# Ordered recurrence: the first chunk's preparation goes inside the hand-ordered part, its inverse and its operand from DRAM are emitted later, and the planner's delays get longer

## The chip, the cores and the metric

The kernel runs on one core of one Trainium2 chip. The metric is the device time of one execution in microseconds (us), smaller is better. In the profile the engines are PE (TensorE matmuls) and PEld (its weight loads), DVE (VectorE), ACT (ScalarE), POOL (GpSimd) and SP (SyncE, which here issues most DMAs).

## The reference: two layers of a hybrid trunk

512 latent tokens and 256 context tokens of width 1024 pass two layers. Layer 0 mixes tokens with four mLSTM heads and eight RWKV-7 heads, layer 1 with RG-LRU and neighbourhood attention; a squared-ReLU MLP follows each mixer. The change touches only RWKV-7 of layer 0, which the reference writes as a scan over single tokens, in both directions z:

```
S = S * w_t + (S a_t) b_t + v_t k_t      # 64 x 64 state of one head
y_t = S r_t
```

w, k, b come from the input projection through low-rank maps; context runs first and its last state starts the latent scan.

## The kernel before: how the work is tiled and ordered

Channels lie on the 128 partitions, tokens along the free dimension. A product with a weight matrix (`gemm`, L290) takes weight tiles of 128x1024, split in a high part `wh` (ACT, L283) and a low part `wl` (POOL or DVE, L287) of the fast matmul type; each output block `psg` is 24 matmuls (xh.wh, xl.wh, xh.wl). `psg` has two PSUM banks in this stage.

**The scan in chunks.** RWKV-7 is computed in 12 chunks of 64 tokens (4 of context, 8 of latent), all 8 heads and both directions at once. A chunk s is prepared, without the state, by two generators:

- `front(s)` (L934) loads `bk`, `ar`, `AS`, `X` from DRAM and forms the chunk's 64x64 products in `psA`, from which ACT and DVE write `AB`, `AS`, `Q`.
- `back(s)` (L968) inverts the unit triangular matrix of each head and direction. Its 16x16 diagonal blocks go through DRAM (`AB` to `dA`, L975; `dA` to `M`, L981), 15 elimination steps of two operations each run on them (L995, L997; on POOL for s up to 4, on DVE for the later ones), and the blocks go out and back in another layout (`Xi` to `invD`, L1000; `invD` to `Xr`, L1002). DVE transposes `Xr` to `Xt` (L1005). Four groups of small matmuls `psI` then merge the 16x16 inverses to 64x64 (`dd`, `t2`, `t3`, `d1`, `T`).

`step(s)` (L1076) carries the state over one chunk with four groups of matmuls `psC`, and `chain` (L1068) calls it for s = 0 to 11.

**The order of the work.** Up to L1276 a scheduler with a modelled clock orders every engine. In this first part the last action before the ordered part is letter "R" of a string (L1224), after which mLSTM head 3 still has two pieces to run. Under "R" the kernel before calls `front(0)` and `back(0)` to the end, so that chunk 0 is prepared among the instructions of head 3, with one PSUM bank for `psA`.

The ordered part (from `ordered[0] = True`, L1276) fixes the order of PE by hand. The main generator `fillers` issues large products: `rwkv_in(1)`, the 15 input projections of the latent tokens, with the four `operands` generators that turn them into the scan's operands; then half of the latent output projection, the context's gate and output projection, and the context MLP. After each matmul a planner's clock `now` is advanced by the matmul's planned time (`mm`, L170), and `poll` (L139) lets any generator whose due time has come emit its next piece: `chain` in queue "step", `prepare(1)` and `prepare(0)` in queues "odd" and "even", `operands` in "in", the context gate in "gate". A generator's `yield 3.0` means: due again 3.0 us of `now` later; a `yield lambda` means: due when the condition holds. A pair of conditions orders the chunks: `front(s)` starts when `keys[0] == s - 1` and enough steps are done (`free`, L1058), and chunks 4 and later wait for `"in"`, the end of `rwkv_in(1)`. The ordered part ends when step 11 has been emitted; what is left of the context MLP then runs beside the last gate.

Only PE follows this order. ACT, DVE, POOL and the DMA queues are ordered by the scheduler's modelled clock, each runs strictly in that order, and an instruction whose operand is late holds all behind it.

Of the kernel before, what the change touches and what calls it, by code (L numbers as in the profile page):

```python
# [14 lines left out]
ALU = mybir.AluOpType  # L15
# [3 lines left out]
P = 128  # L19
# [11 lines left out]
NCR = T // CR  # L31
# [86 lines left out]
def hybrid_kernel(ctx: ExitStack, tc: tile.TileContext, A, out):  # L118
# [623 lines left out]
    def rwkv_in(si, psp, psh, tag, last=None, tail=None):  # L742
# [5 lines left out]
        with tc.tile_pool(name=nm("pha"), bufs=1) as pha, tc.tile_pool(name=nm("ph"), bufs=1) as ph, \  # L748
# [34 lines left out]
            def operands(p, T):  # L783
# [12 lines left out]
                    ups.append((uh, ul))  # L796
                sq = pha.tile([P, n], F32, tag="sq", name=nm("sq"))
                nc.scalar.activation(c64(sq), k, AF.Square, scale=V["k_k"][:, p:p + 1])
                yield 4.2
                pst = psh.tile([P, nb, 2], F32, tag=tag, name=nm("pst"))  # L800
                for c in range(nb):
                    mm(pst[:, c, :], sq[:, P * c:P * c + P], C["hsel"])
# [4 lines left out]
                rx = ph.tile([P, nb, P], F32, tag="sh", name=nm("rx"))  # L807
                nc.scalar.copy(rx.rearrange("p c (h i) -> p (c h) i", h=2),
                               rk.rearrange("p c h -> p (c h)")[:, :, None].to_broadcast([P, 2 * nb, 64]))
                yield 2.6  # L810
                bc = psh.tile([P, nch, 64], F32, tag=tag, name=nm("psbc"))
                for c in range(nb):
                    mm(bc[:, 2 * c:2 * c + 2, :], rx[:, c, :], ident)
# [2 lines left out]
                for z in range(2):  # L816
                    uh, ul = ups[z]
                    for kind in range(2):
                        yield 1.2
                        pw = psh.tile([P, nch, 64], F32, tag=tag, name=nm("psw"))  # L820
                        mm(fl(pw), uh[:, kind, :], low[kind][z], True, False)
                        mm(fl(pw), ul[:, kind, :], low[kind][z], False, True)
                        t_ = ph2.tile([P, nch, 64], F32, tag=f"th{kind}", name=nm("th"))
                        o = 8 * z + 4 * kind + p
                        nc.scalar.activation(t_, pw, AF.Tanh, scale=0.5, bias=DV["upb"][:, o:o + 1])
                        th.append(t_)
# [107 lines left out]
    def front(s):  # L934

        ch = chunk_of(s)
        si, s0 = (0, 0) if s < 4 else (1, 4)
        pr2, X = set_of(s), new_x(s)
        ar = pr2.tile([P, 2, 4, P], F32, tag="ar", name=nm("ar"))
        bk = pr.tile([P, 2, 4, P], F32, tag="bk", name=nm("bk"))  # L940
        Q = pr2.tile([P, 2, 4, 2, 64], F32, tag="Q", name=nm("Q"))
        AS = pr2.tile([P, 2, 4, 2, 64], F32, tag="AS", name=nm("AS"))
        AB = pr.tile([P, 2, 4, 64], F32, tag="AB", bufs=2, name=nm("AB"))
        nc.sync.dma_start(bk, bkD[si][:, s - s0])
        nc.sync.dma_start(ar, arD[si][:, s - s0])
        for q in range(2):
            nc.sync.dma_start(AS[0:64, :, :, q, :], arD[si][hs_[q], s - s0, :, :, 0:64])
        for z in range(2):
            c = 64 * (ch[z] - s0)
            nc.sync.dma_start(X[64:P, z].rearrange("t p q i -> t (p q i)"), vD[si][c:c + 64].rearrange("t p i -> t (p i)"))  # L950
        yield 13.0 if s == CT // CR else 9.0
        for z in range(2):

            pa_ = [None, None]
            for heads in (((0, 1),) if banks["A"][2] > 1 else ((0,), (1,))):
                for q in heads:
                    pa_[q] = bank("A", [P, 4, P])
                for p in range(4):
                    for q in heads:
                        mm(pa_[q][:, p, :], bk[hs_[q], z, p, :], ar[hs_[q], z, p, :])  # L960
                for q in heads:
                    nc.scalar.copy(AB[hs_[q], z], pa_[q][0:64, :, 0:64])
                    nc.vector.tensor_tensor(AS[64:P, z, :, q, :], pa_[q][64:P, :, 0:64], amask(z, 0, HI), op=ALU.mult)
                    nc.vector.tensor_tensor(Q[:, z, :, q, :], pa_[q][:, :, 64:P], amask(z, 1, FULL), op=ALU.mult)
            yield 3.0
        FRONT[s] = (ar, bk, Q, AS, AB, pr2)

    def back(s):  # L968
# [17 lines left out]
        for z in range(2):  # L986
            pt = bank("A", [P, 4, P])
            for p in range(4):
                transpose(pt[:, p, :], bk[:, z, p, :])
            nc.scalar.copy(BK[:, z], pt)  # L990
        eng = nc.gpsimd if s <= CT // CR else nc.vector
        for j in range(15):
            n, m = 15 - j, j + 1
            t_ = tm[:, 0:n, 0:m]
            eng.tensor_tensor(t_, M[:, m:16, j:j + 1].to_broadcast([64, n, m]),  # L995
                              Xi[:, j:j + 1, 0:m].to_broadcast([64, n, m]), op=ALU.mult)
            eng.tensor_tensor(Xi[:, m:16, 0:m], Xi[:, m:16, 0:m], t_, op=ALU.add)  # L997
        for k in range(4):
            dst = bass.AP(tensor=dX.tensor, offset=dX.offset + 512 * k + 16 * (k % 2), ap=[[2048, 16], [32, 16], [1, 16]])
            nc.sync.dma_start(dst, Xi[16 * k:16 * k + 16])  # L1000
        Xr = pr.tile([P, 8, 32], F32, tag="Xr", bufs=2, name=nm("Xr"))
        nc.sync.dma_start(Xr, dX.rearrange("u p t -> p u t"))  # L1002
        Xt = pr.tile([P, 8, 32], F32, tag="Xt", bufs=2, name=nm("Xt"))
        fl8 = lambda a: a.rearrange("p a b -> p (a b)")
        nc.vector.transpose(fl8(Xt), fl8(Xr))  # L1005
        keys[0] = s
        yield 33.0
        yield lambda: merged[0] == s - 1

        tt = (Xt[:, 0:4], Xr[:, 4:8])  # L1010
# [5 lines left out]
                    mm(pi[b32[g], z, p, :], AB[b32[g], z, p, b32[g % 2]], ti[z][b32[g], p, :], tile=(g, g))  # L1016
        dd = pr.tile([P, 2, 4, 32], F32, tag="dd", name=nm("dd"))
        nc.vector.tensor_tensor(dd, pi, lmask, op=ALU.mult)
        yield 1.4
        pj = bank("I", [P, 2, 4, 32])  # L1020
        for z in range(2):
            for p in range(4):
# [8 lines left out]
        T = pr2.tile([P, 2, 4, 64], F32, tag="T", name=nm("T"))  # L1031
        for b in range(2):
            nc.scalar.activation(T[:, :, :, b32[b]], t2, AF.Copy, scale=C["bsel"][:, b:b + 1])
        yield 2.4
        pi = bank("I", [P, 4, 32])
        for p in range(4):
            for z, q in ((0, 0), (1, 0), (0, 1), (1, 1)):
# [1 line left out]
                mm(pi[b32[o], p, :], AB[b32[g], z, p, b32[1 - z]], t3[b32[g], z, p, :], tile=(g, o))  # L1039
        d1 = pr.tile([P, 4, 32], F32, tag="d1", name=nm("d1"))  # L1040
        nc.scalar.copy(d1, pi)
        yield 1.2
        pj = bank("I", [P, 4, 32])
        for p in range(4):
            for z, q in ((0, 0), (1, 0), (0, 1), (1, 1)):
# [4 lines left out]
            nc.vector.scalar_tensor_tensor(t_, pj, C["bsel"][:, z:z + 1], t_, op0=ALU.mult, op1=ALU.add)  # L1050
        tt = (T[:, 0], T[:, 1])
        merged[0] = s
        yield 2.0
        PRE[s] = (ar, GE[:, s], Q, AS, BK, tt)

    seen = set()
# [3 lines left out]
        return steps[0] >= s - (1 if s <= CT // CR else 2) and (s < CT // CR or "in" in done)  # L1060

    def prepare(parity):
        for s in range(2 - parity, NCR, 2):
            yield lambda: free(s) and keys[0] == s - 1
            yield from front(s)
            yield from back(s)

    def chain(S):  # L1068
        for s in range(NCR):
            yield lambda: s in PRE and (s < CT // CR or "lat" in done)  # L1070
            S = yield from step(s, new_x(s), S, new_x(s + 1) if s + 1 < NCR else None)
            rwkv_norms(s)
            steps[0] = s + 1
            yield 3.6

    def step(s, X, S0, Xn):  # L1076
        ar, ge, Q, AS, BK, tt = PRE.pop(s)
        chunk = chunk_of(s)
        pR = bank("C", [P, 2, 4, 64])
        for z, p, q in UNITS:  # L1080
            mm(pR[hs_[q], z, p, :], AS[:, z, p, q, :], X[:, z, p, q, :])
        r_ = pr.tile([P, 2, 4, 64], F32, tag="r", name=nm("r"))
        nc.scalar.copy(r_, pR)
        yield 1.5
        pU = bank("C", [P, 2, 4, 64])
        for z, p, q in UNITS:
            mm(pU[hs_[q], z, p, :], tt[z][hs_[q], p, :], r_[hs_[q], z, p, :])
        nc.scalar.copy(X[0:64, :, :, 0, :], pU[0:64])
        nc.vector.tensor_copy(X[0:64, :, :, 1, :], pU[64:P])
        yield 2.0  # L1090
        S1 = None
        if s < NCR - 1:
            pS = bank("C", [P, 2, 4, 64])
            for z, p, q in UNITS:
                mm(pS[hs_[q], z, p, :], BK[:, z, p, hs_[q]], X[:, z, p, q, :])
            S1 = set_of(s + 1).tile([P, 2, 4, 64], F32, tag="S", name=nm("S"))
            nc.vector.tensor_tensor(S1, pS, S0, op=ALU.add)
            nc.vector.tensor_tensor(S1, S1, ge[:, :, :, None].to_broadcast([P, 2, 4, 64]), op=ALU.mult)
            nc.scalar.copy(Xn[0:64, :, :, 0, :], S1[0:64])
            nc.vector.tensor_copy(Xn[0:64, :, :, 1, :], S1[64:P])  # L1100
        pY = bank("C", [P, 2, 4, 64])
        first = [None, None]
        for z, p, q in UNITS:
            i1 = mm(pY[hs_[q], z, p, :], Q[:, z, p, q, :], X[:, z, p, q, :], first[q] is None, False, shared=True)
            if first[q] is None:
                first[q] = i1
            else:
                after(i1, first[q])
        for z, p, q in UNITS:
            mm(pY[hs_[q], z, p, :], ar[hs_[q], z, p, 64:P], S0[hs_[q], z, p, :], False, False, shared=True)  # L1110
        for z in range(2):
            d = ya_of(chunk[z])
            if chunk[z] in seen:
                nc.vector.tensor_tensor(d, pY[:, z], d, op=ALU.add)
            else:
                seen.add(chunk[z])
                nc.scalar.copy(d, pY[:, z])
        return S1
# [105 lines left out]
    for o in "0000a0c1ccc1cc11c1c22cc2c23c12ccc33cR33":  # L1224
# [3 lines left out]
        elif o == "R":  # L1228
# [5 lines left out]
            pr = st_r.enter_context(tc.tile_pool(name="pr", bufs=1))  # L1234
            add_set()
            inv += [pr.tile([P, 16, 16], F32, name=a) for a in ("M", "Xi", "tm")]
            banks.update(A=(psh2, "h", 1), I=(psa1, "ada", 1))
            S = sets[0].tile([P, 2, 4, 64], F32, tag="S", name="S0")
            nc.vector.memset(S, 0.0)
            nc.vector.memset(new_x(0)[0:64], 0.0)  # L1240
            for _ in front(0):
                pass
            for _ in back(0):
                pass
        else:
            next(work[o], None)
    assert all(next(w, 0) == 0 for w in work.values())
# [373 lines left out]
```

## Time and profile before

| | us |
|---|---|
| median of 3 runs (2118.84 to 2122.49) | 2121.51 |
| the profiled execution's own time | 2113.17 |
| its span, first to last instruction | 2111.3 |
| PE busy (share of the span) | 1932.4 (92%) |
| PEld busy | 1591.6 (75%) |
| DVE busy | 1079.3 (51%) |
| ACT busy | 874.6 (41%) |
| POOL busy | 869.4 (41%) |

Busy time is the union of an engine's instructions. The mean granted clock of PE over the span was 0.956 of full speed. In the list of stretches the ordered part lies from about 406 to 996 us. A number in square brackets at the end of a row is the engine's idle time just before that instruction, and what ended it.

### The profile page before, as it was taken

How to read it: one execution, taken by the hardware profiler on the slowest of the kernel's cores; microseconds unless marked ns; L12 is line 12 of the kernel's file. 1: busy time of each engine (PE TensorE's matmuls, PEld its weight loads, DVE VectorE, ACT ScalarE, POOL GpSimd, SP SyncE). 2: the span in 40 equal slices, each digit the busy share in tenths (PEclk: the TensorE clock that was granted, in tenths of full speed). 3: DMA queues.
4: the chain of work that ended last, by engine and by line, in shares of the span. 5: the costliest groups of instructions: out<-in, count | busy, mean ns of one | idle time of the engine just before them, and what ended most of it. 6: DMA issues, size and time to landing. Idle time of an engine off the chain costs nothing. (4 is left out here: it accounts for less than half of the span.)

```text
span 2111.3 us, 36782 instructions
## 1 busy us (share of the span) xinstructions
PE 1932.4 (92%) x14924; PEld 1591.6 (75%) x14924; DVE 1079.3 (51%) x1947; ACT 874.6 (41%) x1444; POOL 869.4 (41%) x706
## 2 busy tenths in 40 slices
PE   6899997587877889889999999999999999999998
PEld 5788875465656878878877888888666678888887
DVE  6764545268765676676652212234567655122222
ACT  4444544254544434434442323334555655233232
POOL 1456545254435221222434444434454363444444
PEclk9999998698988898999999999999999999999999
DMA  8355657345376454543453233334211032333322
GB/s 307 101 203 201 213 189 238 79 112 152 106 237 187 125 154 134 154 125 111 133 191 124 86 105 95 100 100 152 68 60 41 28 103 70 93 97 100 97 94 80
DMA packets 171929, 271.62 MB, mean 129 GB/s; under 512 B 75056, under 2 KB 113584, under 8 KB 166640
## 3 DMA queue, kind: packets, MB, share of 16 engines
q1 hardware_dynamic: 166704, 263.76, 39.9%
q10 hardware_dynamic: 5056, 5.51, 0.8%
q8 instruction: 118, 1.93, 0.4%
q14 instruction: 51, 0.42, 0.1%
HBM read 244.06 MB, written 25.17 MB: 128 GB/s over the span
## 5 line engine op out<-in xcount | busy, mean ns | idle before, releaser
L287 POOL TENSOR_TENSOR wl<-w,wh 128x1024 fp32r<-128x1024 f32 (+3 forms) x245 | 555.3, 2269 | 816.1 <-PE psg L172 477.5
L283 ACT CAST wh<-w 128x1024 fp32r<-128x1024 f32 (+3 forms) x319 | 313.8, 986 | 527.9 <-PE psg L172 421.0
L172 PE MATMUL psg<-xh,wh 128*128 128x512 f32 (+1 forms) x1440 | 504.3, 364 | 18.6 <-DVE y L385 6.5
L172 PE MATMUL psg<-xl,wh 128*128 128x512 f32 (+1 forms) x1440 | 506.1, 363 | 0.8 <-DVE xl L388 0.7
L172 PEld LDWEIGHTS psg<-xh,wh 128*128 128x128 f32 x1440 | 277.4, 194 | 73.4 <-issue 19.9
L172 PE MATMUL psg<-xh,wl 128*128 128x512 f32 (+1 forms) x1440 | 331.8, 358 | 0.0
L172 PEld LDWEIGHTS psg<-xl,wh 128*128 128x128 f32 x1440 | 279.5, 194 | 46.5 <-issue 7.3
L172 PEld LDWEIGHTS psg<-xh,wl 128*128 128x128 f32 x1440 | 244.4, 192 | 41.4 <-issue 6.8
L172 PE MATMUL psg<-hh,wh 128*128 128x512 f32 (+1 forms) x800 | 267.6, 352 | 6.0 <-DVE res_c L391 3.3
L172 PE MATMUL psg<-hl,wh 128*128 128x512 f32 (+1 forms) x800 | 268.7, 352 | 0.6 <-DVE hl L334 0.6
L391 DVE SCALAR_TENSOR_TENSOR res_l<-psg,mod,res_l 128x512 f32<-128x512 f32 (+1 forms) x108 | 74.2, 689 | 276.6 <-PE psg L172 276.6
L172 PEld LDWEIGHTS psg<-hh,wh 128*128 128x128 f32 x800 | 153.1, 193 | 26.9 <-issue 3.0
L172 PEld LDWEIGHTS psg<-hl,wh 128*128 128x128 f32 x800 | 152.8, 193 | 20.4 <-DVE hl L334 0.8
L172 PE MATMUL psg<-hh,wl 128*128 128x512 f32 (+1 forms) x800 | 166.7, 349 | 0.0
L436 DVE TENSOR_SCALAR r<-psg 128x512 f32<-128x512 f32 (+1 forms) x96 | 57.3, 600 | 179.2 <-PE psg L172 178.8
L172 PEld LDWEIGHTS psg<-hh,wl 128*128 128x128 f32 x800 | 132.9, 191 | 19.1
L334 DVE TENSOR_TENSOR hl<-r,hh 128x512 fp32r<-128x512 f32 (+1 forms) x96 | 93.1, 974 | 86.2 <-ACT hh L333 86.0
L437 ACT ACTIVATE r<-r 128x512 f32<-128x512 f32 (+1 forms) x96 | 53.4, 559 | 133.1 <-DVE r L436 133.1
L287 DVE TENSOR_TENSOR wl<-w,wh 128x1024 fp32r<-128x1024 f32 (+1 forms) x74 | 93.4, 1262 | 29.5 <-ACT wh L283 23.4
L172 PE MATMUL psada<-adaw,sc 128*32 128x256 f32 (+1 forms) x896 | 62.2, 382 | 10.9 <-DMA adaw<-in_ada_w_dram 6.9
L333 ACT CAST hh<-r 128x512 fp32r<-128x512 f32 (+1 forms) x96 | 52.6, 550 | 2.7
L995 POOL TENSOR_TENSOR tm<-M,Xi 64x15 f32<-64x15 f32 (+7 forms) x75 | 26.9, 358 | 62.4 <-DMA M<-dA 57.5
(421 smaller groups left out, 2871.7 us busy)
## 6 DMA issues: line engine op xcount, KB each, us to landing
w<-in_w_dram SPq DMA_DIRECT2D x192, 512.0 KB, 3.6
adaw<-in_ada_w_dram SPq DMA_DIRECT2D x40, 1024.0 KB, 6.9
w<-in_ev_in_dram SPq DMA_DIRECT2D x47, 512.0 KB, 3.7
w<-in_od_in_dram SPq DMA_DIRECT2D x32, 512.0 KB, 3.6
adaw<-in_ada_dram SPq DMA_DIRECT2D x16, 512.0 KB, 11.2
w<-in_out_w_dram SPq DMA_DIRECT2D x32, 256.0 KB, 3.5
ar<-arD SPq DMA_DIRECT2D x12, 512.0 KB, 4.4
bk<-bkD SPq DMA_DIRECT2D x12, 512.0 KB, 5.0
```

The costliest lines, as they stand in the source:

```text
L172: ins = nc.tensor.matmul(o, l, r, start=start, stop=stop, skip_group_check=shared, **kw)
L283: nc.scalar.copy(wh, w)
L287: eng.tensor_tensor(wl, w, wh.bitcast(F32), op=ALU.subtract)
L333: nc.scalar.copy(h, x)
L334: nc.vector.tensor_tensor(l, x, h.bitcast(F32), op=ALU.subtract)
L391: nc.vector.scalar_tensor_tensor(r_, ps, modcol(layer, idx, m, cnd), r_, op0=ALU.mult, op1=ALU.add)
L436: nc.vector.tensor_scalar(r_, ps, 0.0, None, op0=ALU.max)
L437: nc.scalar.activation(r_, r_, AF.Square)
L995: eng.tensor_tensor(t_, M[:, m:16, j:j + 1].to_broadcast([64, n, m]), Xi[:, j:j + 1, 0:m].to_broadcast([64, n, m]), op=ALU.mult)
```

## The change

Eleven delays of the planner get longer, in `operands`, in the merge of `back`, in `front` and in `step`. `front(0)` and `back(0)` are no longer called under "R"; instead queue "even" starts at chunk 0, so that chunk 0 is prepared inside the ordered part like the others, with two banks for `psA` (the branch for one bank goes). In `back`, the single delay of 33 is divided: 8 after the block-transposes of `bk`, then the elimination in three groups of five steps with 3 between them, then 14 before the transpose of `Xr`, and 1 after it. `tc.keep_in_program_order` pins the first operation of each group, and the transpose, behind everything emitted before on the same engine.

```diff
@@ operands @@
-                yield 4.2
+                yield 4.6
...
-                yield 2.6
+                yield 3.6
...
-                        yield 1.2
+                        yield 1.8
@@ front @@
-            yield 3.0
+            yield 3.4
@@ back @@
+        keys[0] = s
+        yield 8.0
         eng = nc.gpsimd if s <= CT // CR else nc.vector
         for j in range(15):
+            if j in (5, 10):
+                yield 3.0
...
-            eng.tensor_tensor(t_, M[:, m:16, j:j + 1]...
+            ins = eng.tensor_tensor(t_, M[:, m:16, j:j + 1]...
+            if j in (0, 5, 10):
+                tc.keep_in_program_order(ins)
...
+        yield 14.0
         Xt = pr.tile([P, 8, 32], F32, tag="Xt", bufs=2, name=nm("Xt"))
-        nc.vector.transpose(fl8(Xt), fl8(Xr))
-        keys[0] = s
-        yield 33.0
+        tc.keep_in_program_order(nc.vector.transpose(fl8(Xt), fl8(Xr)))
+        yield 1.0
         yield lambda: merged[0] == s - 1
...
-        yield 1.4 / 2.4 / 1.2 / 2.0      # the merge's four
+        yield 2.4 / 4.0 / 1.8 / 2.6
@@ prepare @@
-        for s in range(2 - parity, NCR, 2):
+        for s in range(parity, NCR, 2):
@@ chain and step @@
-            yield 1.5 / 2.0 / 3.6
+            yield 2.2 / 3.0 / 4.2
@@ under "R" @@
-            banks.update(A=(psh2, "h", 1), I=(psa1, "ada", 1))
-            for _ in front(0):
-                pass
-            for _ in back(0):
-                pass
```

(The lines with several numbers stand for one line each.)

## Rows read from the trace of the kernel before

**Rows 1.** Stretches: length, busy us (instructions) PE PEld DVE ACT POOL, PEclk, DMA, GB/s.
```profile
340.00:1060.00 720.00, 592.76 (x7485) 514.25 (x7485) 470.03 (x928) 297.67 (x533) 244.86 (x313) 0.89 0.49 143
...
410.00:620.00 210.00, 174.44 (x1831) 134.01 (x1830) 146.67 (x222) 100.26 (x175) 90.22 (x148) 0.90 0.48 141
...
380.00:390.00 10.00, 1.54 (x6) 1.14 (x6) 1.18 (x3) 1.04 (x3) 7.74 (x25) 0.50 0.42 128
390.00:400.00 10.00, 0.29 (x20) 0.29 (x24) 0.31 (x1) 0.00 (x0) 3.89 (x14) 0.50 0.24 46
400.00:410.00 10.00, 7.05 (x225) 6.07 (x217) 2.10 (x7) 1.76 (x4) 0.00 (x0) 0.50 0.04 9
...
450.00:460.00 10.00, 4.94 (x16) 4.27 (x17) 3.25 (x6) 3.56 (x5) 1.33 (x6) 0.67 0.55 126
...
550.00:560.00 10.00, 2.80 (x12) 2.03 (x11) 4.76 (x7) 2.31 (x4) 3.25 (x5) 0.79 0.24 46
```

**Rows 2.** Timeline of PE around chunk 0: start, length, engine, line, operation [idle before].
```profile
327.04 0.58 PE L172 MATMUL psg<-xh,wh 128*128 128x512 f32 x1
...
363.88 1.40 PE L172 MATMUL psA<-ar,bk 64*128 64x128 f32 x8 [2.24 <-issue]
...
381.66 1.54 PE L736 MATMUL pst<-cst,hall 128*128 128x128 f32 x6 [2.27 <-POOL hall L731]
...
399.71 0.65 PE L172 MATMUL psI<-Xr,AB 32*32 32x32 f32 x32 [16.51 <-DMA Xr<-invD]
...
408.08 0.80 PE L172 MATMUL psg<-xl,wh 128*128 128x512 f32 x1
```

**Rows 3.** Timeline of POOL: first and last elimination operation of chunks 0 and 1.
```profile
382.09 0.22 POOL L995 TENSOR_TENSOR tm<-M,Xi 64x15 f32<-64x15 f32 x1 [0.48 <-DMA M<-dA]
...
393.88 0.21 POOL L997 TENSOR_TENSOR Xi<-Xi,tm 64x15 f32<-64x15 f32 x1
...
433.15 0.73 POOL L995 TENSOR_TENSOR tm<-M,Xi 64x15 f32<-64x15 f32 x1 [35.23 <-DMA M<-dA]
...
446.49 0.22 POOL L997 TENSOR_TENSOR Xi<-Xi,tm 64x15 f32<-64x15 f32 x1
```

**Rows 4.** Waits of DVE, 405 to 1060 us: total, times, longest.
```profile
DVE Xt L1005 <- DMA Xr<-invD: 36.6, 10, 8.0
DVE tm L995 <- DMA M<-dA: 18.5, 6, 6.8
```

**Rows 5.** Timeline of DVE: the three longest of these waits.
```profile
453.62 0.45 DVE L1005 STREAM_TRANSPOSE Xt<-Xr 128x256 f32<-128x256 f32 x1 [7.59 <-DMA Xr<-invD]
...
555.10 0.45 DVE L1005 STREAM_TRANSPOSE Xt<-Xr 128x256 f32<-128x256 f32 x1 [7.97 <-DMA Xr<-invD]
...
908.55 0.18 DVE L995 TENSOR_TENSOR tm<-M,Xi 64x15 f32<-64x15 f32 x1 [6.84 <-DMA M<-dA]
```

**Rows 6.** Timeline of PE: the three longest stalls between 420 and 1050 us.
```profile
455.06 2.08 PE L172 MATMUL psbc<-cst,rx 128*128 128x128 f32 x8 [5.24 <-ACT rx L808]
...
559.55 0.79 PE L172 MATMUL psw<-low,uh 128*128 128x512 f32 x1 [7.20 <-ACT th L825]
...
911.89 1.97 PE L172 MATMUL psC<-r,T 64*64 64x64 f32 x32 [5.77 <-ACT r L1083]
```

**Rows 7.** Waits of PE, 420 to 1050 us: total, times, longest.
```profile
PE psI L172 <- DVE dd L1018: 10.5, 4, 3.8
PE psC L172 <- DVE X L1089: 8.2, 4, 3.7
```

**Rows 8.** Timelines of ACT and PE: steps 4 and 6, the last step, the fill's end.
```profile
723.78 0.58 ACT L1083 COPY r<-psC 128x512 f32<-128x512 f32 x1
...
804.16 0.59 ACT L1083 COPY r<-psC 128x512 f32<-128x512 f32 x1
...
995.97 1.15 PE L172 MATMUL psC<-S,ar 64*64 64x64 f32 x32
...
1022.48 0.36 PE L172 MATMUL psg<-hh,wh 128*128 128x256 f32 x1 [1.87 <-ACT xhol L333]
```

## Prediction: what the change does to the time

> **What bounds the kernel now.** The profile's page comes first: PE is busy for 1932 of 2111 us, and all other engines far less. So a change counts only where PE stands idle or runs at its lower clock. The list of stretches tells where that is: outside 340 to 1060 us PE is all but full, and in there it is busy for 593 of 720 us [rows 1]. The largest hole lies at 380 to 410 us [rows 1]: busy 1.5, 0.3 and 7.1 us of 10 each, with the granted clock at 0.50, the lower level (1.2 GHz), throughout. The timeline of PE says what the hole is [rows 2]: the last transposes of mLSTM head 3 end at 381.66 + 1.54 = 383.20; then PE waits 16.51 us for chunk 0's `Xr`, merges chunk 0, and only at 408.08 does the stream of large products go on. Its first matmul ran at 327.04, which shows that the stream's data had long been there: what held it is the fixed order, in which step 0, and so all of chunk 0's inverse, stands behind that one matmul. The second place is the ordered part itself (406 to 996 us), where PE is idle in many short stalls. The waits of DVE and its timeline [rows 4, 5], laid beside PE's [rows 6], show one pattern: DVE stands before a transpose `Xt` until its operand is back from DRAM (36.6 us in ten cases), or before an elimination step until `M` is (18.5 us in six), and PE stalls just then. DVE's 7.59 us up to 453.62 go with PE's 5.24 up to 455.06; 7.97 up to 555.10 with 7.20 up to 559.55; 6.84 up to 908.55 with 5.77 up to 911.89.
>
> All sums are made against the profiled execution (2113.17 us). The median of the runs shown is 2121.51, 8.3 above it; I take the difference over to the median.
>
> **Term 1, chunk 0 into the ordered part: -27 us.** The planner starts chunk 0 and lets the large products flow while its delays run, so the stream need no longer wait for the inverse. How early can it flow? Head 3 ends at 383.20, but chunk 0's `psA` stands in its way: 2.24 us of waiting and 1.40 us of work at 363.88 [rows 2]. Without them, about 379. What is not removed but moved: four groups of `psA`, two of transposes, priced the same, at 1.40, and six of `psI` at 0.65, 12.3 us at the lower clock, some 6 at the upper. So 408 - 379 - 6 = 23. Besides, the planner emits 9 us of products before the first `psA`; like the one at 327.04 they may run among head 3's short waits. I take 4 of the 9: 27. Bounds: head 3 not quicker and nothing early, 408 - 383 - 6 = 19; all early, 383 - 379 + 19 + 9 = 32. If the memory that head 3 frees only at its end holds the products' evacuation up, the two PSUM banks of `psg` still take what is emitted before.
>
> What chunk 0 delays is chunk 1's step and the others of context. One lane's delays add up to 9 + 3.4 + 3.4 + 8 + 3 + 3 + 14 + 1 + 2.4 + 4.0 + 1.8 + 2.6 = 55.6 of the planner's us (before: 9 + 3 + 3 + 33 + 1.4 + 2.4 + 1.2 + 2.0 = 55.0), so step 3 comes later by about the time of a step. It is wanted by the context gate, which is emitted after the latent projection's half; I count 2 us of stall there. Chunks 4 and later wait for the end of `rwkv_in(1)` and not for chunk 0, so they start as before.
>
> **Term 2, `M` and `Xr` waited for by the planner and not by DVE: -22 us.** An elimination step is now emitted 8 planner's us after its transposes, and `Xt` 14 after the last group; pinned, it cannot be put ahead of its data by the scheduler. In the trace `Xr` needs from 393.88 + 0.21 (last step) to 399.7 (first use), 5.6 us [rows 2, 3], well under 14. The three stalls of PE in [rows 6] give 18.2 us, 0.81 of the 22.4 that DVE waited there [rows 5]. The other thirteen waits make 55.1 - 22.4 = 32.7 us [rows 4], 2.5 each; at 0.81 the whole would be 45, but short waits often lie inside PE's slack. I take 18 and an eighth of the 32.7, 22. Bounds: 5 (other late operands hold the same matmuls) and 45.
>
> **Term 3, longer yields: -6 us.** 10.5 us in four waits on `dd` and 8.2 in four on `X` [rows 7]. These yields grow by 1.0 each (1.4 to 2.4, 2.0 to 3.0), filled with other matmuls, and the eight stalls shrink by about that, 8 us; I take 6, since some on `X` also fall under term 2. Bounds: 0 and 18.7, all of both. The cost of the longer yields lies in the chain's length: four lane cycles of 0.6 and a step's 9.4 - 7.1 = 2.3 make 5 planner's us, or 7 us at the rate of the trace (from step 4 to step 6, 804 - 724 = 80 us, for a cycle of 55 in delays) [rows 8]. The fill that is left covers it: the last step's matmuls end at 997, the context MLP still runs at 1022 [rows 8], 25 us later. Were that cover gone, it would cost 7. The `operands` delays grow from 11.6 to 15.4 per block of 128 channels; the two projections that follow each, and half a projection behind the last, run meanwhile.
>
> **Term 4, the clock: -6 us.** At 450 to 460 us the clock is 0.67, with PE busy for 4.94 us; at 550 to 560 it is 0.79 [rows 1]. Each long stall is followed by matmuls at the lower level; 0.33 x 4.94 = 1.6 us for the first. Four such places: 6. Bounds: 0 and 13, if eight such places go.
>
> **Term 5, what gets worse: +13 us.** `Xt` is now only 1 us ahead of the matmuls that read it, and pinned behind all the DVE work emitted before. DVE was up to 3.8 us late for `dd` in 4 of 12 cases [rows 7], after a yield of 1.4; the same lateness on `Xt` is 4 x 1.5 to 12 x 3.8 us, 6 to 46; I take 6, the value by the cases counted. The elimination of chunk 0 ran on POOL while DVE was all but idle (1.2 and 0.3 us of 10, [rows 1]), in 394.1 - 382.1 = 12.0 us; chunk 1's, in the stretch where DVE is busy for 147 of 210 us [rows 1], took 446.7 - 433.2 = 13.5 us, its first operation 0.73 instead of 0.22 [rows 3]. Chunks 0 to 4 all run so now, with 29 planner's us from the block-transposes to the merge where 33 were; I count 5 for a late `Xr` there (0 to 5 x 4 = 20). With the gate's 2 that makes 13; 6 to 68 at the ends.
>
> A sentence on the rule for this: the Trainium skill ("SBUF — State Buffer", section "Who interferes with whom") says that a DVE instruction with two SBUF inputs and a GpSimd instruction that reads SBUF hold a port against each other for their whole length. The 0.73 against 0.22 agrees in direction. By the rule taken to its end, each of the 30 operations waiting once for 0.5 us, chunk 0's elimination would take 12 + 15 = 27 us, and its `Xr` would still lie within the 20 planner's us from its first step to the transpose, or 29 us of trace, but for some 4 us.
>
> **Sum:** -27 - 22 - 6 - 6 + 13 = -48. 2113.2 - 48 = 2065 for the profiled execution, 2121.5 - 48 = 2073.5 for the median.
>
> **Rivals.**
> - *Only the hole closes.* The stalls move: PE waits for `Xt` or `Xr` where DVE waited before, term 5 at 34 eats terms 2 to 4. For it: DVE's 147 of 210 us, so something is often late. Against: the longest stalls stand so exactly behind waits for DMAs. -27: 2094; 2085 to 2105.
> - *All the relief is had.* Terms 1 to 4 at 32, 38, 10 and 10, near their ends, term 5 at its low end of 6: -84, 2037. For it: stalls and lower clock go together. Against: every stall would have to go without a successor.
> - *Slower: the chain outlasts the fill.* If chunk 0's latency is passed on through the lanes to step 11, the chain ends later by a whole cycle, 80 us at the trace's rate. The fill covers 25; for 55 us PE would run the chain alone. Against that stand term 1 and half of term 2, 38: +17, 2138. It decides from the point where the chain is more than 25 + 38 = 63 us late. For it: each lane is full from chunk 4 on. Against: chunks 4 and 5 wait for `rwkv_in(1)`, which is not later in the planner's order than chunk 0's own 6 us.
> - *It does not do what it says.* The stream still stands, since PE's order puts chunk 0's `psA` behind head 3 and something late behind that; relief and new waits cancel. 2121.
>
> **How the numbers follow.** Forecast 0.52 (its own range 2053 to 2085), only the hole 0.21, all the relief 0.12, no change 0.06, slower 0.09. A change under 0.2% (4.2 us) can't be told from none here. Faster: 0.52 + 0.21 + 0.12 = 0.85; same 0.06; slower 0.09. The range, 2034 to 2113, leaves out the far half of the full relief (0.05), no change and slower (0.15).
>
> **What would show it.** Term 1: no wait of PE near 16 us after head 3, `psg` of the latent projections running from about 379 us on, and step 0's `r` not before some 60 us after that. Term 2: DVE's waits for `Xr` and `M` in the ordered part under 15 us together instead of 55. Term 3: PE's waits on `dd` and `X` at half. Term 5: new rows of PE waiting for `Xt` or `Xr`. The forecast is wrong if step 11 ends after the context MLP, or if PE's idle time in the ordered part has not fallen.

## The result: 2120.18 to 2072.32 us, and the profile after

The changed kernel takes 2072.32 us (median of 4 runs, 2069.68 to 2074.5), the kernel before 2120.18 on the same chip (median of 4, 2114.92 to 2122.49). The ratio is 0.9777, with an interval of 0.9754 to 0.98. The forecast was 2073.5. The profiled span fell from 2111.3 to 2067.9, PE's granted clock over it rose from 0.956 to 0.967.

The list of stretches shows where the 43.4 us of span went. Each kernel is cut at the same events: head 3 ends, (before only) the stream goes on, the context MLP starts, the first product on `xhol` starts (near the context MLP's end), the end. Columns as in [rows 1].

```profile
318.00:383.20 65.20, 45.80 (x311) 33.72 (x309) 37.90 (x102) 27.79 (x64) 30.30 (x46) 0.80 0.72 215
383.20:408.08 24.88, 5.42 (x225) 4.82 (x225) 3.10 (x8) 1.90 (x5) 9.28 (x34) 0.50 0.19 51
408.08:694.19 286.11, 229.53 (x2241) 181.24 (x2239) 191.78 (x325) 130.16 (x233) 120.41 (x195) 0.89 0.52 152
694.19:1026.91 332.72, 296.32 (x4661) 279.20 (x4662) 232.98 (x499) 135.00 (x231) 83.33 (x46) 0.93 0.48 136
1026.91:2111.30 1084.39, 1063.98 (x5250) 853.08 (x5248) 425.81 (x623) 435.08 (x635) 479.27 (x263) 0.99 0.30 95
```

```profile
318.00:376.98 58.98, 41.95 (x295) 31.31 (x293) 39.33 (x95) 27.44 (x60) 29.18 (x41) 0.90 0.72 226
376.98:650.47 273.49, 221.87 (x2464) 175.99 (x2463) 191.84 (x327) 130.00 (x238) 131.57 (x232) 0.90 0.59 164
650.47:977.88 327.41, 289.78 (x4686) 273.67 (x4686) 221.18 (x506) 133.05 (x228) 78.81 (x45) 0.95 0.49 136
977.88:2067.90 1090.02, 1065.43 (x5224) 850.91 (x5224) 429.62 (x626) 437.17 (x638) 483.17 (x265) 0.99 0.30 95
```

The first fence is before, the second after. Head 3 ends 6.2 us earlier, the hole of 24.9 us is gone, the next two stretches give 12.6 and 5.3, and the last takes 5.6 back. PE's timeline after, at the places of [rows 2], [rows 6] and [rows 8]:

```profile
375.44 1.54 PE L736 MATMUL pst<-cst,hall 128*128 128x128 f32 x6 [10.82 <-POOL hall L731]
377.82 2.08 PE L172 MATMUL psA<-ar,bk 64*128 64x128 f32 x16 [0.83 <-issue]
379.83 3.11 PE L172 MATMUL psg<-xh,wl 128*128 128x512 f32 x7
...
453.69 0.65 PE L172 MATMUL psI<-Xr,AB 32*32 32x32 f32 x32 [7.64 <-DMA Xr<-invD]
...
916.64 0.65 PE L172 MATMUL psI<-Xr,AB 32*32 32x32 f32 x32 [13.15 <-DMA Xr<-invD]
...
961.72 1.15 PE L172 MATMUL psC<-S,ar 64*64 64x64 f32 x32
...
969.97 1.12 PE L172 MATMUL psg<-hh,wl 128*128 128x256 f32 x8
```

Chunk 0's `psA` now follows head 3 at once, with no wait like the 16.51 us of [rows 2], and the stream goes on at 379.83. But head 3's own last transposes wait 10.82 us for `hall`, where they waited 2.27 before. And there are new stalls on `Xr`, one of 13 us, and the last step (961.72) starts only 8 us ahead of the context MLP's last products (969.97). The waits of PE and DVE between 360 and 1010 us answer to [rows 4] and [rows 7]:

```profile
PE psI L172 <- DMA Xr<-invD: 24.9, 4, 13.1
PE psI L172 <- DVE Xt L1009: 6.0, 3, 3.4
PE psI L172 <- DVE dd L1021: 2.1, 1, 2.1
PE psC L172 <- DVE X L1092: 1.4, 1, 1.4
DVE Xt L1009 <- DMA Xr<-invD: 10.3, 4, 4.1
```

DVE's waits for `Xr` and `M` fell from 55.1 to 10.3 us, PE's for `dd` and `X` from 18.7 to 3.5; 30.9 us of PE waits for `Xr` and `Xt` are new. So PE gained little idle time back in the ordered part: in the two stretches up to the first product on `xhol` it is idle for 93.0 us before (56.6 and 36.4) and for 89.3 after (51.6 and 37.6). The other 14.2 us that they lost are busy time, at a higher granted clock (0.89 to 0.90, 0.93 to 0.95); chunk 0's work came into them, some of the stream's went out.

### The profile page after: what moved, and what is told of

The parts are those of the page before. It is cut to its first block, busy times and chain, and to the rows that moved or that the text cites. A ratio compares the mean times of both kernels' runs of the same rounds, so it can differ in the third digit from the quotient of the medians.

```text
span 2067.9 us, 36790 instructions
## 1 busy us (share of the span) xinstructions
PE 1910.0 (92%) x14924; PEld 1571.0 (76%) x14924; DVE 1071.8 (52%) x1947; ACT 873.9 (42%) x1444; POOL 871.0 (42%) x706
## 5 line engine op out<-in xcount | busy, mean ns | idle before, releaser
L172 PE MATMUL psg<-xl,wh 128*128 128x512 f32 (+1 forms) x1440 | 499.9, 359 | 2.2 <-DVE xl L388 2.1
L387 ACT ACTIVATE xh<-y,mod 128x256 fp32r<-128x256 f32 (+1 forms) x56 | 32.0, 598 | 39.2 <-DVE y L385 38.7
```

Source lines behind the costliest of these rows:

```text
L172: ins = nc.tensor.matmul(o, l, r, start=start, stop=stop, skip_group_check=shared, **kw)
L387: nc.scalar.activation(xh[:, k, :], y, AF.Identity, bias=s)
```

## The experiments

Each ratio is to the kernel before, run beside it on the same chip (so 0.01 is 21 us); letters in the expectations are names of theories. First the three parts alone.

**Chunk 0 alone** (the kernel before with it):

```diff
-        for s in range(2 - parity, NCR, 2):
+        for s in range(parity, NCR, 2):
...                                          # under "R"
-            for _ in front(0): pass
-            for _ in back(0): pass
```

> Only the first part of the change: chunk 0 is prepared inside the ordered part; the single delay of 33, the old delays and the unpinned order stay. Theory A (what the two profiles suggest: head 3 ends 6 us earlier, the 25 us after it go, 10 us of products run before it, 6 us of chunk 0's matmuls are added): -35 us, about 2085. Theory B (the prediction's term 1): -27, about 2093. Rival C (the parts need each other: without the later operand, chunk 0 too makes DVE stand before its transpose and PE behind it): -15 to -25, about 2100.

Measured: 2089.56 us, ratio 0.9874 (0.9859 to 0.9889): -26.7 us. DVE's waits stay as in [rows 4]: 38.9 us for `Xr`, 15.1 for `M`. Term 1 was right in size. Head 3 ends at 381.75, 1.4 us earlier than before.

**The back part alone** (chunk 0 still under "R"): the 33 split into 8, 3, 3, 14 and 1, the first operation of each group and the transpose pinned. These sum up to 29, so a lane's delays are 51.0 instead of 55.0.

```diff
-        nc.vector.transpose(fl8(Xt), fl8(Xr))
-        yield 33.0
+        yield 14.0
+        tc.keep_in_program_order(nc.vector.transpose(fl8(Xt), fl8(Xr)))
+        yield 1.0
...                  # and 8 before, 3 within the elimination, pinned
```

> Only the second part: elimination emitted 8 later and in three groups, the transpose 14 later, both pinned; chunk 0 stays before the ordered part and all other delays stay. Theory B (prediction's term 2 less its term 5): -22 + 11 = about -11, 2109. Theory A (the old waits are replaced by PE's own wait for the operand): -3 to -8, 2113. Rival C (pins alone cost as much as they save): 0, 2120.

Measured: 2079.36, ratio 0.9826 (0.981 to 0.9843): -36.8 us, far more than priced. From head 3's end to the first product on `xhol`, before and then this kernel (columns as above):

```profile
383.20:1026.91 643.71, 531.28 (x7124) 465.26 (x7124) 427.86 (x831) 267.07 (x468) 213.02 (x275) 0.90 0.48 140
```

```profile
382.68:989.49 606.81, 511.09 (x7124) 446.94 (x7124) 421.25 (x830) 263.27 (x466) 209.08 (x275) 0.93 0.52 148
```

For the same 7124 matmuls PE is idle for 95.7 us instead of 112.4, and busy for 20.2 us less. Busy time times clock, as an estimate of work done, is about the same (531.3 x 0.90 = 478, 511.1 x 0.93 = 475), so by this estimate the shorter busy time is the clock's. Of the 36.9 us, 16.7 are idle time and 20.2 busy time. PE's own waits for the operand, from 410 us on, are 8.4 us on `Xr` and 0.5 on `Xt`:

```profile
PE psI L172 <- DMA Xr<-invD: 8.4, 3, 6.1
```

**The eleven longer delays alone** (with a line more, so that the planner's clock also goes on where its queues hold only conditions):

```diff
-                yield 4.2 / 2.6 / 1.2          # operands
+                yield 4.6 / 3.6 / 1.8
-            yield 3.0 | 1.4 / 2.4 / 1.2 / 2.0  # front | merge
+            yield 3.4 | 2.4 / 4.0 / 1.8 / 2.6
-            yield 3.6 / 1.5 / 2.0              # chain, step
+            yield 4.2 / 2.2 / 3.0
```

> Only the third part: the eleven longer delays, with the single delay of 33 kept, so that a lane's cycle is 59.6 instead of 55.0; the planner's loop gets one line so that it does not stop when the last chunk is emitted after the fill. Theory B (prediction's term 3): -6 for the stalls, and the chain longer by 4 x 4.6 x 1.45 = 27 us, just the fill that is left: about 2115. Theory A (the longer delays pay only with the shorter wait in the back part): the chain outlasts the context MLP, +5 to +15, about 2130.

Measured: 2128.23, ratio 1.0064 (1.0038 to 1.009): 13.5 us slower (8 to 19). The last step now ends after the fill, as PE's timeline shows:

```profile
1003.83 1.11 PE L173 MATMUL psg<-hh,wl 128*128 128x256 f32 x8
...
1011.61 1.70 PE L173 MATMUL psC<-S,ar 64*64 64x64 f32 x32
```

Added up the three parts give -26.7 - 36.8 + 13.5 = -50.0, against -47 for the whole change. This doesn't show that the parts leave each other alone: as the last part added, the delays cost more (next run).

**The whole change with the old delays** (the diff just shown, backwards):

> The changed kernel with the eleven old delays, so chunk 0 inside and the back part split, a lane's cycle of 51.0. Theory B (term 3): 6 us slower than the changed kernel, 2078. Theory A (delays and new waits cancel, but the chain ends earlier): 2072 within 4. Rival C (the longer delays are what keeps PE from waiting in the merge and in the step): 10 to 20 us slower, 2085 to 2090.

Measured: 2048.39, ratio 0.9686 (0.9666 to 0.9706), span 2043.6: 24 us faster than the changed kernel by the medians, 19 by the ratios. PE's timeline at the last step and at the fill's end, to be laid beside 961.72 and 969.97 above:

```profile
930.88 1.15 PE L172 MATMUL psC<-S,ar 64*64 64x64 f32 x32
...
964.60 1.13 PE L172 MATMUL psg<-hh,wl 128*128 128x256 f32 x8
```

33.7 us of fill stand behind the last step, where the changed kernel has 8.3. From the end of the fill to the end of the span it is 2043.6 - 965.7 = 1077.9 us, there 2067.9 - 971.1 = 1096.8, 18.9 more. Where these lie is seen when the stretch is cut at the first matmul behind the latent projection (`psst`, at 987.86 and 1009.14). The changed kernel, then this one:

```profile
971.09:1009.14 38.05, 29.74 (x225) 22.79 (x225) 22.84 (x31) 15.02 (x25) 15.16 (x12) 0.91 0.35 116
```

```profile
965.73:987.86 22.13, 21.55 (x95) 17.49 (x94) 10.95 (x15) 10.63 (x17) 10.17 (x7) 1.00 0.38 120
```

15.9 of the 18.9 us lie here: PE is idle for 8.3 us instead of 0.6, its clock is 0.91 instead of 1.00, and 4.2 us are the output norm's `psy` matmuls, which this kernel has run within its fill.

**What in the back part works.** From here on each kernel is the last one (called the base) with one edit. Without the four pins:

```diff
-            if j in (0, 5, 10):
-                tc.keep_in_program_order(ins)
...
-        tc.keep_in_program_order(nc.vector.transpose(fl8(Xt), fl8(Xr)))
+        nc.vector.transpose(fl8(Xt), fl8(Xr))
```

> The kernel with chunk 0 inside, the back part split and the old delays (2048), without the four pins per chunk. Theory D (the scheduler would float a transpose or an elimination step ahead of its data, so the pins carry the gain): DVE's waits on M and Xr come back to 30 to 50 us and the time to 2065 to 2080. Rival E (emitting them later is enough, the pins only fix what stands there anyway): 2048 within 4.

Measured: 2073.0, ratio 0.9796 (0.9776 to 0.9816), 23 us slower than the base. DVE waits nearly as in [rows 4], though all is emitted as late as in the base:

```profile
DVE Xt L1007 <- DMA Xr<-invD: 32.5, 11, 6.4
DVE tm L996 <- DMA M<-dA: 18.5, 6, 4.9
```

So later emission without the pins does not take these waits away. It is not without effect, though: chunk 0 alone, with the undivided 33, stood at 0.9874, this kernel stands at 0.9796, the base at 0.9686. Some 16 us come without the pins (later emission, a lane shorter by 4, or both; not separated), 23 with them.

The elimination emitted at once and unpinned, only the transpose later and pinned:

```diff
-        yield 8.0
...
-            if j in (5, 10):
-                yield 3.0
...              # no pin on the elimination
-        yield 14.0
+        yield 28.0
```

> The same kernel (2048) with the elimination emitted at once, in one piece and unpinned, as before the change; only the transpose is emitted later (28 after it, so that the lane's cycle stays at 51.0) and pinned. Theory D (the wait for Xr was the larger part, 36.6 of 55.1 us, and the elimination's grouping the smaller): half to two thirds of the back part's gain stays, 2058 to 2066. Rival E (grouping does nothing): 2048 within 4. Rival F (the elimination in one block on DVE is what stops the merge): 2070 to 2080.

Measured: 2076.17, ratio 0.9814 (0.9787 to 0.984). The waits on `M` are back (23.3 us in seven), those on `Xr` half back (14.9 in three). So holding the transpose alone gives no more than holding neither; both places have to be held.

**Which delay costs.** The three of `operands` alone (4.6, 3.6, 1.8):

> The same kernel (2048) with the three longer delays of the operands alone, which belong to no lane. Theory G (the 24 us that the eleven delays cost come from the chain's length against the fill): 2048 within 4. Rival H (they delay the end of the input projections and with it chunk 4): 2055 to 2065.

Measured: 2065.29, ratio 0.9759 (0.9735 to 0.9782). The fill behind the last step is no shorter (42.8 us); the context MLP starts later, at 668.02 instead of 650.52. DVE's timeline shows a cause:

```profile
566.92 1.76 DVE L846 TENSOR_TENSOR bk<-th,cs 128x512 f32<-128x512 f32 x1
568.61 0.67 DVE L1134 TENSOR_REDUCE ms<-sq 128x8 f32<-128x512 f32 x1
569.64 0.20 DVE L1136 RECIPROCAL ms<-ms 128x8 f32<-128x8 f32 x1 [0.37 <-ACT ms L1135]
569.88 0.69 DVE L1137 TENSOR_TENSOR ya_c<-ya_c,ms 128x512 f32<-128x512 f32 x1
570.49 0.44 DVE L1009 STREAM_TRANSPOSE Xt<-Xr 128x256 f32<-128x256 f32 x1
```

and PE's the price:

```profile
570.98 0.65 PE L172 MATMUL psI<-Xt,AB 32*32 32x32 f32 x32 [9.60 <-DVE Xt L1009]
```

The pinned transpose stands behind 13 us of nearly unbroken DVE work (operands and the output norm). In the base it follows the same norm at 558.66, and PE has no stall on it there; but there PE stands for `xhom`:

```profile
558.34 0.80 PE L172 MATMUL psg<-xhom,wh 128*128 128x512 f32 x1 [10.67 <-ACT xhom L333]
```

With the longer `operands` that wait is 7.91 us. The two waits together cost 6.8 us more than in the base, of the 17.5 us by which the context MLP is late; the rest is not explained.

The lane alone, 18.6 where 14 stood (55.6 planner's us, the sum in the changed kernel):

> The same kernel (2048) with the wait before the transpose at 18.6 instead of 14.0, so that a lane's cycle is 55.6 as in the changed kernel, with all eleven old delays. Theory G (length of the lane decides: the last step comes some 27 us later and the context MLP is all but used up when the latent gate needs cover): 2066 to 2074. Rival H (it is where the longer delays stand, in the merge and the steps, not the length): 2044 to 2052, as the operand is even safer.

Measured: 2079.84, ratio 0.9822 (0.98 to 0.9843). The late operand is now `Xt` (PE's waits):

```profile
PE psI L172 <- DVE Xt L1009: 38.1, 7, 8.4
```

The merge's four and `front`'s (also 55.6):

> The kernel with chunk 0 inside, the back part split and the old delays (2048), with the five longer delays of front and merge alone: a lane's cycle is 55.6 again. Theory G (the lane's length costs by leaving too little fill behind the last step, wherever it is put): last step near 960, the latent gate without cover, 2066 to 2080. Rival H (the 18.6 cost because the transpose was late in DVE's order, and longer merges rather save waits): 2040 to 2052.

Measured: 2070.29, ratio 0.9782 (0.9737 to 0.9827): that is the changed kernel's time. The three of `chain` and `step`:

> The same kernel (2048) with the three longer delays of the step alone, 9.4 instead of 7.1 per step, which lie on no lane. Theory G: the last step 3 us later, within the fill, 2046 to 2052. Rival H (waits on r and X shrink): 2040 to 2046. Rival I (any shift of the planner's order costs 10 to 20 us, as the operands' delays did): 2058 to 2068.

Measured: 2062.38, ratio 0.9752 (0.9714 to 0.9789); a wait of 8.17 us on `dd` at 574.83 and a context MLP from 667.98 on, as with `operands`. The lane shorter, 11 where 14 stood:

> e4_olddelays with the yield before Xt at 11 instead of 14, so that one lane's delays add up to 48.0 instead of 51.0; all else as in e4_olddelays. Theory G (the lane's length costs time: in e8_lane 4.6 more gave +31 us): 3.0 less makes the chain end earlier, the last step before the 930.88 of e4_olddelays, and the kernel 5 to 20 us faster than e4_olddelays, ratio 0.960 to 0.966 to the kernel before. Theory I (e4_olddelays is a good order by chance, and any shift of the order costs 14 us or more, as the three longer operands delays and the three longer step delays did): 10 to 25 us slower than e4_olddelays, ratio 0.973 to 0.981, with no earlier last step or a later one. Theory K (the 14 is needed: with 11 Xr is late again): the waits of DVE on Xr in the ordered part, 4.8 us in two cases in e4_olddelays, rise over 12 us, and PE's waits on Xr and Xt together from 13.0 to over 25; ratio 0.970 to 0.98.

Measured: 2082.01, ratio 0.9846 (0.9805 to 0.9888), slower by 34 us. `Xr` is late again, theory K (waits of DVE, then of PE):

```profile
DVE Xt L1009 <- DMA Xr<-invD: 26.7, 8, 5.2
```

```profile
PE psI L172 <- DMA Xr<-invD: 17.7, 7, 6.0
PE psI L172 <- DVE Xt L1009: 11.5, 2, 9.6
```

With the timelines of all these kernels the cost of a short fill can be laid out. First the fill left behind the last step (start to start), then the time from the fill's end to the span's, then the part of it up to `psst`, behind the latent projection:

| kernel | fill left, us | rest, us | up to `psst`, us |
|---|---|---|---|
| eleven longer delays alone | -7.8 | 1114.3 | 53.6 |
| the changed kernel | 8.3 | 1096.8 | 38.1 |
| lane longer (18.6) | 15.3 | 1092.7 | 35.0 |
| merge and front longer | 20.6 | 1090.0 | 30.2 |
| steps longer | 32.8 | 1083.0 | 22.1 |
| before | 33.3 | 1080.9 | 21.9 |
| base | 33.7 | 1077.9 | 22.1 |
| operands longer | 42.8 | 1082.0 | 22.1 |
| lane shorter (11) | 45.8 | 1083.1 | 22.1 |

From 32.8 us on, more fill gives nothing; at 20.6 and less, the way to `psst` takes 8 to 31 us more than the base's, in the first two rows with work in it that the others have done within the fill. How much fill is enough lies between these two rows. Behind `psst` it is 1055.7 to 1060.9 us in all nine, with no order by the fill.

**The elimination on POOL for all chunks:**

```diff
-        eng = nc.gpsimd if s <= CT // CR else nc.vector
+        eng = nc.gpsimd
```

> The same kernel (2048) with the elimination on POOL for all chunks, where it is on DVE for chunks 5 to 11. Theory J (DVE is the engine whose order holds the merge up from 650 us on; 7 x 30 operations of 0.21 us leave it): waits on dd, t, Xt fall, 2035 to 2045. Rival K (POOL needs 12 to 14 us for it, so Xr comes after the planner's 20, and each of 7 chunks stops PE for some us): 2052 to 2075.

Measured: 2032.86 (2027.87 to 2035.51), ratio 0.9607 (0.9569 to 0.9644): faster than both kernels, and 15.5 us than the base. The stretch from the context MLP's start to its end, the base and then this kernel:

```profile
650.52:965.73 315.21, 287.47 (x4687) 269.86 (x4688) 238.44 (x519) 133.83 (x232) 84.14 (x49) 0.97 0.52 144
```

```profile
652.81:946.14 293.33, 281.61 (x4687) 266.42 (x4688) 177.71 (x309) 134.41 (x232) 150.32 (x244) 0.99 0.55 155
```

Here the whole gain lies: 21.9 us, of which 4.4 are given back before and behind (the span falls by 17.5), with DVE busy for 61 us less. PE's waits on `Xr` (8.4 us in the base) are gone. What an elimination on DVE meets is to be seen in the changed kernel, ahead of its 13 us stall. POOL's timeline, then DVE's:

```profile
881.75 2.37 POOL L287 TENSOR_TENSOR wl<-w,wh 128x1024 fp32r<-128x1024 f32 x1 [7.80 <-ACT wh L283]
890.85 2.70 POOL L287 TENSOR_TENSOR wl<-w,wh 128x1024 fp32r<-128x1024 f32 x1 [6.73 <-ACT wh L283]
899.13 2.41 POOL L287 TENSOR_TENSOR wl<-w,wh 128x1024 fp32r<-128x1024 f32 x1 [5.58 <-ACT wh L283]
```

```profile
882.72 1.44 DVE L996 TENSOR_TENSOR tm<-M,Xi 64x15 f32<-64x15 f32 x1
...
891.21 2.40 DVE L996 TENSOR_TENSOR tm<-M,Xi 64x48 f32<-64x48 f32 x1
893.65 0.20 DVE L1000 TENSOR_TENSOR Xi<-Xi,tm 64x48 f32<-64x48 f32 x1
...
899.46 2.16 DVE L996 TENSOR_TENSOR tm<-M,Xi 64x60 f32<-64x60 f32 x1
...
910.13 0.40 DVE L1000 TENSOR_TENSOR Xi<-Xi,tm 64x15 f32<-64x15 f32 x2
```

An operation of 0.2 us takes 2.40, and ends when POOL's `wl` ends (891.21 + 2.40 = 893.61; 890.85 + 2.70 = 893.55); so do the two others (884.16 and 884.12, 901.62 and 901.54). With that, and with the rest of DVE's work and the next chunk's steps in between, this chunk's elimination runs from 882.72 to 910.3, 27.6 us; the three waits are 5.4 of them. On POOL a late chunk of the last kernel took 14.7:

```profile
838.51 0.22 POOL L996 TENSOR_TENSOR tm<-M,Xi 64x15 f32<-64x15 f32 x1 [9.60 <-DMA M<-dA]
...
843.91 1.18 POOL L1000 TENSOR_TENSOR Xi<-Xi,tm 64x55 f32<-64x55 f32 x1
...
853.03 0.21 POOL L1000 TENSOR_TENSOR Xi<-Xi,tm 64x15 f32<-64x15 f32 x1
```

Over the seven late chunks it is 14.1 to 22.0 us on POOL (mean 16.8), and 15.0 to 34.9 on DVE in the changed kernel (22.6). The rule of the Trainium skill ("SBUF — State Buffer", section "Who interferes with whom") that the prediction weighed, a port that each of the two engines holds against the other for a whole instruction, agrees with these rows. It works both ways: the prediction let POOL's short operations wait for DVE, and in the last kernel 14 of them take 1.1 to 1.4 us, each ending within 0.2 us of the end of a `wl` on DVE (1.35 us from 843.56 on, beside the middle row above); DVE's short ones take up to 2.45 us beside POOL's longer `wl`. But that is not what makes DVE the worse place. A single operation took 0.30 us on the mean on DVE in the changed kernel and 0.33 on POOL in the last one; and in the kernel before, where the elimination was emitted in one piece, DVE took 11.6 to 20.4 us for it (mean 15.4), with operations of up to 2.3 us in six of the seven chunks. The operations' own time is 9.0 of the 22.6 us and 9.4 of the 15.4; what is longer is the time between them, with the groups apart and pinned behind DVE's other work. Whether the gain comes from that or from the 61 us of which DVE is freed was not separated.

## Why the prediction came out right, and which steps did not

The total (-48 forecast, -47 by the ratio) is right by luck: two errors of about 20 us cancel.

**Term 1 (-27)** is right in its sum: -26.7 alone. Its marks are there: the stream at 379.83 where 379 was named, and step 0's `r` at 444.11, 64 us later. Its parts are not. Without `psA` head 3 was to end 4 us earlier; alone it ended 1.4 earlier, since PE then waits 10.8 us for `hall` in the same place. In its stead all of the early products ran ahead of head 3's end (40 more matmuls of the stream, 9 us), of which 4 us were counted.

**Term 3 (-6) is the step that failed, in its sign.** The eleven delays cost 13.5 us alone, and about 19 (by the ratios) to 24 us (by the medians) as the last part added. "The fill that is left covers it" was put against a chain 7 us longer. The waits on `dd` and `X` did shrink, by 15 us, but the fill left is 8.3 where it was 33.3, and 33.7 with the old delays: the chain moved by 25 us against it. The 7 came from a comparison of the lane's sums, 55.0 before and 55.6 after. But with the old delays the lane has 51.0, in more pieces, and leaves 33.7, as the 55.0 of before did. That each piece is emitted a little later than it is due, so that four more pieces make up for the missing 4, would explain it; this is argued, not shown. Nor is a fill that still outlasts the chain enough cover: with 8.3 us of it the way to `psst` took 15.9 us longer than with 33.7. The rest of the 24 us lies ahead of the fill's end (5.4, with the 4.2 us of `psy` not yet done there) and behind `psst` (3.0).

**Terms 2, 4 and the part of 5 that belongs to `back`** were too small: -22 and +11, and what the clock gives, against -36.8 measured. By the estimate above, most of what was short is the clock: PE's idle time fell by 16.7 us where -11 was priced, and its busy time by 20.2 where 6 was priced for the clock. The new waits of PE on `Xr` and `Xt` are 8.9 us in that run, near the 11 priced; the 30.9 of the whole change come with the longer delays (13.0 with the old ones).

**What the marks missed.** In the whole change DVE's waits (10.3 us, under the 15 named) and PE's on `dd` and `X` (3.5 of 18.7) went as forecast. But PE's idle time in the ordered part, the sign that counts, fell only by 3.7 us: PE waits for `Xr` itself now. With the old delays it is 76.7 us instead of 89.3.

**The rivals.** That the chain outlasts the fill is real: the delays alone do it (-7.8 us of fill). The price named for it, a whole cycle, was too large.

**What stays open.** The costs of the delays don't add: `operands` 17, merge and front 22, steps 14, all together 24. Any shift of the planner moves DVE's order. Whether the pinned `Xt` lands behind a burst decides over some 10 us (9.60 at 568 to 571 us, with `operands` longer and with the shorter lane; with the longer steps it is `dd`, 8.17). If the base lies on the good side of that by chance, differences of 10 to 20 us from it by any single edit are partly this; no run tests it. Open too is what gave the 16 us of the divided back part without pins, and what the elimination on POOL gains by.

## What to carry to other kernels

A wait that an in-order engine makes for a DMA went away here when the instruction was both emitted later and pinned; emission alone left the waits as they were, and a pin can put the instruction behind a burst. A wait that leaves one engine can come back on another: what counts is the idle time of the engine that bounds the kernel. A delay "hidden" by a fill is paid from the fill that the work behind it needs: measure how much must be left, here more than 20.6 and no more than 32.8 us, before lengthening a chain. A total that comes out right says little: run the parts alone.

## What the runs showed of the hardware

DVE's 0.2 us operations on SBUF took up to 2.45 us beside one POOL operation on 128x1024, and ended within 0.1 us of it (all eleven over 1 us in the changed kernel). The same operations on POOL, 0.2 to 0.4 us, took up to 1.44 us beside one such operation on DVE, and ended within 0.2 us of it (14 cases). Thirty of them took 14.1 to 22.0 us on POOL; on DVE 11.6 to 20.4 in one piece, and 15.0 to 34.9 divided and pinned behind other work.
